# The final norm of an expert layer, moved beside the experts and added to an output that holds the bias

## The chip, the core and the metric

One core of one Trainium2 chip runs the whole program. The time is the device time of one execution in microseconds; the kernel before took 1721.29 us (median of three runs, 1720.49 to 1723.58). A core has TensorE (PE, with its weight loads as PEld), VectorE (DVE), ScalarE (ACT), GpSimd (POOL) and SyncE (SP), each with a queue of its own, and 16 DMA engines that serve the queues of SP and POOL here.

## The reference

One decoder layer over 1024 tokens of 1024 values. An attention mixer and a first layer norm give `h`; then a mixture of experts and a second layer norm give the output. Only the last part matters here:

```python
h   = layer_norm(ALPHA * h + mix, ln1_g, ln1_b)
lg  = h @ w_coarse + b_coarse          # 4 groups, the best one is taken
lf  = h @ w_fine[grp] + b_fine         # 8 experts of that group, the best 2 are taken
ffn = sum over the 2 experts of weight * ((silu(h @ w_gate[e]) * (h @ w_up[e])) @ w_down[e])
out = layer_norm(ALPHA * h + ffn, ln2_g, ln2_b)
```

So both experts of a token lie in one group of eight: experts 0 to 7, 8 to 15, 16 to 23 or 24 to 31. A token of group 0 has its whole sum once expert 7 is through.

## The kernel before

The attention and the first norm end near 1050 us. The routing (`out_norm`, `out_route`, `out_rank`, `out_table`, lines 1259 to 1360) writes `h` to `hbuf` and to `ybuf`, and a table in DRAM with the rows and weights of each expert; `idx` is the table read back.

Then 32 experts run one after the other (loop at line 1676), each in 12 steps `k`. An expert takes up to 128 rows. Steps 0 to 7 multiply the rows by 1024 x 1024 gate and up weights, steps 8 to 11 by 512 x 1024 down weights; a step is one weight tile of 128 x 1024. Each float32 tile is split in two: `eh` is a rounded copy (ACT, line 1479) and `el` the remainder (DVE, line 1480); six matmuls per step (line 1497) use `eh` twice and `el` once. The rows are gathered from `hbuf` by POOL (`gather`, line 1372), transposed on PE (line 1460) and split in the same way (`xt`, ACT line 1466, DVE line 1467). After step 7 come `silu` and `turn`: ACT's silu of each half (line 1504), DVE's product (line 1505), PE's transposes (line 1514), ACT's and DVE's split (lines 1516, 1517). After step 11 `put` scales the two banks on ACT (lines 1521, 1522) and POOL adds the rows to `ybuf` by an indirect DMA (line 1523).

PE, DVE, ACT and POOL take their instructions in program order (`MAN`, line 1668). SP's queue is ordered by the framework, which lets a load go ahead when its page is free. `fetch` takes pages from a ring of some 44 (`er`), in which a tile's page serves first for the load and then for its `el`; `prep` (line 1474) makes `eh` and `el` up to three steps ahead, with three buffers for `eh`. `split_rows` of the next expert and `ahead` come behind the matmuls of a step.

The final norm is a list of letters (`TAIL`, line 65; `final`, line 1630). After expert 30 eight blocks of 128 tokens are loaded from `ybuf`; after the last step of expert 31 they are normed by DVE, ACT and POOL together, and written, with the rows of expert 31 left out. Those are gathered, the expert's product is added (`last_add`, line 1625), normed (`finish_rows`, line 1540) and scattered to the output (`put_rows`, line 1549). The gain and bias are spread over the partitions by matmuls during experts 28 and 29 (`final_gb`, line 1558). A loop behind it (line 1713) takes blocks of rows beyond 128 of an expert; here it has no passes.

Of the kernel before, what the change touches and what calls it, by code (L numbers as in the profile page):

```python
# [9 lines left out]
FP = mybir.dt.float32  # L10
FR = mybir.dt.float32r
BF = mybir.dt.bfloat16
# [51 lines left out]
GBL = (22, 0)  # L64
TAIL = {(30, 11): "L0 L1 L2 L3 L4 L5 L6 L7", (28, 2): "K", (28, 4): "K", (29, 2): "K", (29, 4): "K", (31, 9): "P", (31, 11): "S0 V01 S1 N01 U0 A3 S2 V13 D2 G0p A5 S4 N13 V35 R D4 U1 B0p N35 G1p E2 H4 D5 B1p A7 Z A6 V58 U3 G3p D7 N58 E5 U6 G6p E7 B3d C6p F X"}
# [11 lines left out]
def tile_hybrid(ctx: ExitStack, tc: tile.TileContext, x, xT, w_t, w_gate, pos_k, w1_k, w2_k, pos_v, w1_v, w2_v,  # L77
# [744 lines left out]

    ybd = dram.tile([4, 128, 1024], FP, name="ybd")
# [339 lines left out]
    nof, tok8 = (rc_pool.tile([128, NB], FP, name=n) for n in ("nof", "tok8"))  # L1163
    nid = rc_pool.tile([128, NB], I32, name="nid")
    nc.gpsimd.iota(tok8, pattern=[[128, NB]], base=0, channel_multiplier=1, allow_small_or_imprecise_dtypes=True)
# [14 lines left out]
    tab = dram.tile([S * NE, 2], I32, name="tab")  # L1180
    ti = h_pool.tile([128, 512], I32, name="ti", tag="z", bufs=NZ)
    nc.vector.memset(ti, 4096)
    nc.sync.dma_start(tab.rearrange("(p n) c -> p (n c)", p=128), ti)

# [101 lines left out]
    def out_route(b, L):  # L1286
# [8 lines left out]
        nc.vector.tensor_scalar(e4, e4, sc_[:, 1:2], None, op0=OP.is_equal)  # L1295
        nc.vector.tensor_scalar(e4, e4, -1.0, 1.0e30, op0=OP.add, op1=OP.mult)
# [21 lines left out]
        nc.vector.tensor_tensor(nof[:, b:b + 1], oh[:, 0, NE - 1:NE], oh[:, 1, NE - 1:NE], op=OP.add)  # L1318
# [94 lines left out]

    nc.vector.scalar_tensor_tensor(nid, nof, 4096.0, tok8, op0=OP.mult, op1=OP.add)
# [12 lines left out]
    nc.vector.tensor_copy(ntot, CX[:, 31:32])  # L1427
# [112 lines left out]
    def finish_rows(pl, z, o, g2, b2):  # L1540

        def centre(mean):
            nc.vector.scalar_tensor_tensor(o, z, mean, g2, op0=OP.subtract, op1=OP.mult)
        r, _, _ = stats(pl, z, EPS / ALPHA ** 2, centre, ((0, 512), (512, 1024)))
        for i in range(2):
            c = slice(i * 512, i * 512 + 512)
            nc.vector.scalar_tensor_tensor(o[:, c], o[:, c], r, b2[:, c], op0=OP.mult, op1=OP.add)

    def put_rows(o, ids, outs=()):
        s_ = nc.gpsimd.indirect_dma_start(out=out[0], out_offset=bass.IndirectOffsetOnAxis(ap=ids, axis=0), in_=o,  # L1550
                                          in_offset=None, bounds_check=S - 1, oob_is_err=False)
# [4 lines left out]
    zs = {}  # L1556

    def final_gb():

        kept.extend([next(er_at) for _ in range(3)])  # L1560
        gb, *ts = (p(n) for p, n in zip(kept, ("gb", "g2", "b2")))
        for i, src in enumerate((ln2_g, ln2_b)):
            nc.sync.dma_start(gb[32 * i:32 * i + 1, :], bass.AP(tensor=src.tensor, offset=src.offset,
                                                              ap=[[0, 1], [1, 1024]]))
        yield
        for i, t in enumerate(ts):
            for h in range(2):
                c, ps = slice(h * 512, h * 512 + 512), bank("pt")
                nc.tensor.matmul(ps, ones[32 * i:32 * i + 1, :], gb[32 * i:32 * i + 1, c], start=True, stop=True)
                nc.scalar.copy(t[:, c], ps)  # L1570
                yield ts

    def final_load(b):
        zs[b] = er("zf")
        nc.sync.dma_start(zs[b], ybuf[b * 128:b * 128 + 128, :])

    def final_stats(b):
        bs = fmt[:, b, 2:14].rearrange("p (a b) -> p a b", a=2)
        for i in range(2):
            nc.vector.bn_stats(bs[:, i], zs[b][:, i * 512:i * 512 + 512])  # L1580
        nc.vector.bn_aggr(fmt[:, b, 0:2], fmt[:, b, 2:14])

    def final_stats_act(b):

        os_[b] = er("of")
        mean, var, s1 = fmt[:, b, 0:1], fmt[:, b, 1:2], fmt[:, b, 2:3]
        nc.scalar.activation(os_[b], zs[b], AF.Copy, scale=1.0 / D, accum_out=mean)
        nc.scalar.activation(os_[b], zs[b], AF.Square, scale=-1.0, bias=mean, accum_out=s1)
        nc.scalar.activation(var, s1, AF.Copy, scale=1.0 / D)

    def final_root(a, n):
        root(fmt[:, a:n], *(fmv[:, i, a:n] for i in range(3)), EPS / ALPHA ** 2)

    def final_newton(a, n):
        newton(fmt[:, a:n], *(fmv[:, i, a:n] for i in range(4)))

    def final_unit(b):
        nc.scalar.activation(zs[b], zs[b], AF.Identity, scale=fmv[:, 1, b:b + 1], bias=fmv[:, 3, b:b + 1])

    def final_shift(b):  # L1600
        nc.vector.scalar_tensor_tensor(zs[b], zs[b], fmt[:, b, 0:1], gb[0], op0=OP.subtract, op1=OP.mult)

    def final_scale(b, skip=False):
# [4 lines left out]
    def final_gain(b, eng):  # L1608
        eng.tensor_tensor(zs[b], zs[b], gb[0], op=OP.mult)
# [220 lines left out]
```

## Time and profile before

| what | us |
| --- | --- |
| median of the runs | 1721.29 |
| the execution that was profiled | 1719.97 |
| its span, first to last instruction | 1718.2 |
| busy: PE, DVE, ACT, POOL | 1587.5, 1264.3, 1103.8, 439.2 |
| granted TensorE clock, mean | 0.972 |

The profile is one execution taken by the hardware profiler. Times in a row are us from the start of the span; "busy" is the time in which an engine executes. A row of the timeline gives start, duration, engine, line, operation, output and inputs with their shapes, and in brackets how long the engine had stood idle and what released it. Instructions that follow one another closely are one row with a count, and their durations overlap a little, so the distance of the starts is the better price of one. Tiles that share a bank of PSUM carry each other's names: `pt` and `av` at line 1497 are the two banks of gate and up, `sc` those of the down product.

### The profile page before, as it was taken

The numbers are of one execution on the slowest core, as the hardware profiler recorded it, in microseconds if no ns is written. First come the engines' busy times: TensorE is split into PE (matmuls) and PEld (weight loads), VectorE is DVE, ScalarE is ACT, GpSimd is POOL, SyncE is SP. The second block draws the span as 40 slices with busy tenths as digits, with TensorE's granted clock in tenths as the row PEclk, the third lists the DMA queues.
The fourth block names the chain that finished last, engine by engine and source line by source line (L and its number), as shares of the span: only waits on it lengthen the run. The fifth ranks groups of instructions, "written<-read, shape, count | busy, mean of one in ns | idle before, by whom it ended". The sixth has DMA issues, their size and how long they took to land. (4 is left out here: it accounts for less than half of the span.)

```text
span 1718.2 us, 24639 instructions
## 1 busy us (share of the span) xinstructions
PE 1587.5 (92%) x8114; PEld 1310.5 (76%) x8114; DVE 1264.3 (74%) x2680; ACT 1103.8 (64%) x2037; POOL 439.2 (26%) x390
## 2 busy tenths in 40 slices
PE   7999999998899999999799996999999999999970
PEld 6888888777678988788678895777777777777750
DVE  5555553347867774588877797998998899889786
ACT  4566665525557785578933014887887888788772
POOL 1011122341223332323610242221121212113134
PEclk9999999999999999999999997999999999999995
DMA  4111112232320111001356769999999999999532
GB/s 172 38 37 38 37 38 68 74 101 89 123 86 35 36 47 33 25 18 57 96 177 212 292 213 346 353 364 358 362 366 354 367 359 329 370 364 370 164 118 102
DMA packets 104518, 308.85 MB, mean 180 GB/s; under 512 B 20387, under 2 KB 24611, under 8 KB 104388
## 3 DMA queue, kind: packets, MB, share of 16 engines
q1 hardware_dynamic: 94228, 289.25, 46.0%
q0 software_dynamic: 10160, 18.00, 4.2%
q8 instruction: 65, 1.06, 0.3%
q14 instruction: 65, 0.53, 0.1%
HBM read 283.18 MB, written 41.17 MB: 189 GB/s over the span
## 5 line engine op out<-in xcount | busy, mean ns | idle before, releaser
L1480 DVE TENSOR_TENSOR el<-er,eh 128x1024 fp32r<-128x1024 f32 x384 | 448.1, 1219 | 31.7 <-ACT eh L1479 29.8
L1479 ACT CAST eh<-er 128x1024 fp32r<-128x1024 f32 x384 | 391.0, 1056 | 43.8 <-PE pt L1497 29.1
L232 PE MATMUL pp<-xh,wh 128*128 128x512 f32 x672 | 273.7, 407 | 1.6 <-DVE q L287 1.6
L234 PE MATMUL pp<-xh,wl 128*128 128x512 f32 x672 | 265.9, 396 | 0.0
L233 PE MATMUL pp<-xl,wh 128*128 128x512 f32 x672 | 264.4, 393 | 0.0
L1497 PE MATMUL av<-eh,xt 128*128 128x512 f32 x512 | 196.9, 395 | 1.4 <-ACT xt L1466 1.2
L1497 PE MATMUL pt<-eh,xt 128*128 128x512 f32 x512 | 196.2, 393 | 0.0
L1523 POOL DMA_INDIRECT ybuf<-y,idx x30 | 95.9, 3198 | 212.3 <-ACT y L1522 205.6
L234 PEld LDWEIGHTS pp<-xh,wl 128*128 128x128 f32 x672 | 127.1, 189 | 29.7
L232 PEld LDWEIGHTS pp<-xh,wh 128*128 128x128 f32 x672 | 127.5, 190 | 21.1 <-DVE q L287 2.0
L233 PEld LDWEIGHTS pp<-xl,wh 128*128 128x128 f32 x672 | 127.7, 190 | 19.4
L1497 PE MATMUL sc<-eh,at 128*128 128x512 f32 x512 | 141.4, 398 | 0.0
L892 POOL TENSOR_TENSOR pw<-pw,st 128x64 f32<-128x64 f32 (+5 forms) x128 | 85.9, 701 | 183.2 <-DVE st L887 156.5
L1497 PEld LDWEIGHTS av<-eh,xt 128*128 128x128 f32 x512 | 96.4, 188 | 27.8 <-ACT eh L1479 3.0
L1497 PEld LDWEIGHTS pt<-eh,xt 128*128 128x128 f32 x512 | 96.5, 189 | 22.2
L930 DVE TENSOR_TENSOR PT<-pt,PT 128x512 fp32r<-128x512 f32 (+1 forms) x136 | 90.9, 671 | 25.1 <-ACT PT L929 23.6
L1497 PEld LDWEIGHTS sc<-eh,at 128*128 128x128 f32 x512 | 93.6, 188 | 20.1 <-ACT eh L1479 0.4
L1497 PE MATMUL av<-el,xt 128*128 128x512 f32 x256 | 104.6, 409 | 0.0
L1497 PE MATMUL pt<-el,xt 128*128 128x512 f32 x256 | 100.9, 394 | 0.0
L1372 POOL DMA_INDIRECT xg<-hbuf,idx x31 | 33.3, 1075 | 253.3 <-PE pp L1460 239.6
L123 POOL TENSOR_TENSOR wl<-wr,wh 128x1024 fp32r<-128x1024 f32 x24 | 59.0, 2458 | 140.1 <-ACT wh L122 120.5
L929 ACT CAST PT<-pt 128x512 fp32r<-128x512 f32 (+1 forms) x136 | 76.7, 567 | 16.7 <-PE pt L922 15.0
(431 smaller groups left out, 3586.0 us busy)
## 6 DMA issues: line engine op xcount, KB each, us to landing
er<-in_w_gu_dram SPq DMA_DIRECT2D x256, 512.0 KB, 7.7
er<-in_w_dn_dram SPq DMA_DIRECT2D x128, 512.0 KB, 7.2
wr<-in_w_t_dram SPq DMA_DIRECT2D x44, 512.0 KB, 3.3
mgd<-mg SPq DMA_DIRECT2D x32, 256.0 KB, 2.0
G<-mgd SPq DMA_DIRECT2D x32, 256.0 KB, 3.4
xr<-in_xT_dram SPq DMA_DIRECT2D x8, 512.0 KB, 8.7
wo<-in_w_oT_dram SPq DMA_DIRECT2D x8, 512.0 KB, 4.8
wor<-in_w_out_dram SPq DMA_DIRECT2D x8, 512.0 KB, 7.6
```

What stands on the lines that cost most here:

```text
L123: (eng or nc.vector).tensor_tensor(lo, raw, hi.bitcast(FP), op=OP.subtract)
L232: nc.tensor.matmul(ps, wh[:, kk], xh[k][:, c], start=k == 0, stop=False)
L233: nc.tensor.matmul(ps, wh[:, kk], xl[k][:, c], start=False, stop=False)
L234: nc.tensor.matmul(ps, wl[:, kk], xh[k][:, c], start=False, stop=k == 7)
L892: nc.gpsimd.tensor_tensor(t, t, st[:, 1, hi_, i:i + 1].to_broadcast([128, w]), op=OP.mult)
L929: nc.scalar.copy(t[:, 0], src)
L930: nc.vector.tensor_tensor(t[:, 1], src, t[:, 0].bitcast(FP), op=OP.subtract)
L1372: nc.gpsimd.indirect_dma_start(out=t, out_offset=None, in_=hbuf, in_offset=bass.IndirectOffsetOnAxis(ap=ids, axis=0), bounds_check=S - 1, ...
L1479: nc.scalar.copy(wh, r)
L1480: nc.vector.tensor_tensor(wl, r, wh.bitcast(FP), op=OP.subtract)
L1497: nc.tensor.matmul(pss[h], a[j == 1][:, kk], (wl if j == 2 else wh)[:, h], start=o == 0 and j == 0, stop=o == n - 1 and j == 2)
L1523: nc.gpsimd.indirect_dma_start(out=ybuf, out_offset=bass.IndirectOffsetOnAxis(ap=self.ids, axis=0), in_=y, in_offset=None, bounds_check=S ...
```

## The change

The tokens of a group are normed as soon as its experts are through, in blocks of up to 128 rows, while later experts run. A list of the rows of each group is made in expert 1 (`lists`): a count by matmul, eight scatters into a table `tabf`, one load `idf`. Groups 0 to 2 have three blocks each, which begin at the experts in `FIN`; group 3 has two blocks and the rows of expert 30, all normed during expert 31 (`last_roots`, `last_ends`); the rows of expert 31 are normed at the end as before. Every block is spread over hooks of the step loop: `at(i, f)` runs `f` behind step `i`. A block that begins at expert e gathers its rows at step 8 of expert e - 1, takes the mean and the sum of squares on ACT at steps 4 and 6 of expert e, and has its root at step 8: three small DVE operations for a first guess from the bits, then fourteen on POOL. ACT's scaling comes at step 4 of expert e + 1, DVE's product with the gain in two halves at step 6 of experts e + 1 and e + 2. The bias is not added by an engine: eight DMAs write it to every row of the output beforehand, and the scatter of a block adds to it. The rows of experts 30 and 31 are written whole. `kept` takes three pages of the ring in expert 1 and no more in expert 22.

```diff
+NFB = 3, 3, 3, 2
+FIN = {9: (0, 0), 11: (0, 1), 13: (0, 2), 17: (1, 0), 19: (1, 1), 21: (1, 2), 25: (2, 0), 26: (2, 1), 28: (2, 2)}
...
+    for b in range(NB):
+        nc.sync.dma_start(out[0, b * 128:b * 128 + 128, :], bass.AP(tensor=ln2_b.tensor, offset=ln2_b.offset,
+                                                                    ap=[[0, 128], [1, 1024]]))
...
+    def lists():
+        kept.extend([next(er_at) for _ in range(3)])
+        gb[:] = (p(n) for p, n in zip(kept, ("g2", "b2", "any")))
+        for t, src in zip(gb, (ln2_g, ln2_b)):
+            nc.sync.dma_start(t, bass.AP(tensor=src.tensor, offset=src.offset, ap=[[0, 128], [1, 1024]]))
...
+        put = []
+        for b in range(NB):
+            s_ = nc.gpsimd.indirect_dma_start(out=tabf, out_offset=bass.IndirectOffsetOnAxis(ap=at[:, b:b + 1], axis=0),
+                                              in_=nid[:, b, :], in_offset=None, bounds_check=128 * 32 - 1,
+                                              oob_is_err=False)
...
+        nc.sync.dma_start(idf.rearrange("p n c -> p (n c)"), tabf.rearrange("(p n) c -> p (n c)", p=128))
...
+    def fin_mean(z, f):
+        nc.scalar.activation(gb[2], z, AF.Copy, scale=1.0 / D, accum_out=f[:, 0:1])
+
+    def fin_square(z, f):
+        nc.scalar.activation(gb[2], z, AF.Square, scale=-1.0, bias=f[:, 0:1], accum_out=f[:, 1:2])
...
+    def fin_bits(f):
+
+        v, r, t, n = (f[:, i:i + 1] for i in range(2, 6))
+        b = t.bitcast(I32)
+        nc.vector.tensor_scalar(v, f[:, 1:2], 1.0 / D, VE, op0=OP.mult, op1=OP.add)
+        nc.vector.tensor_scalar(b, v.bitcast(I32), 1, None, op0=OP.logical_shift_right)
+        nc.vector.tensor_scalar(r.bitcast(I32), b, -1.0, float(0x5f3759df), op0=OP.mult, op1=OP.add)
+        for _ in range(3):
+            nc.gpsimd.tensor_tensor(t, r, r, op=OP.mult)
+            nc.gpsimd.tensor_tensor(t, t, v, op=OP.mult)
+            nc.gpsimd.tensor_scalar(t, t, -0.5, 1.5, op0=OP.mult, op1=OP.add)
+            nc.gpsimd.tensor_tensor(r, r, t, op=OP.mult)
+        nc.gpsimd.tensor_tensor(t, f[:, 0:1], r, op=OP.mult)
+        nc.gpsimd.tensor_scalar(n, t, -1.0, 0.0, op0=OP.mult, op1=OP.add)
...
+    def fin_unit(z, f):
+        nc.scalar.activation(z, z, AF.Identity, scale=f[:, 3:4], bias=f[:, 5:6])
+
+    def fin_gain(z, c):
+        nc.vector.tensor_tensor(z[:, c], z[:, c], gb[0][:, c], op=OP.mult)
...
+    def take(ids):
+        b = dict(z=er("zf"), f=fin_new())
+        rows_of(b["z"], ids)
+        return b
+
+    def block(n, ids):
+
+        b = {}
+        at(n - 4, lambda: b.update(take(ids)))
+        at(n + 4, lambda: fin_mean(b["z"], b["f"]))
+        at(n + 6, lambda: fin_square(b["z"], b["f"]))
+        at(n + 8, lambda: fin_bits(b["f"]))
+        at(n + 16, lambda: fin_unit(b["z"], b["f"]))
+        at(n + 18, lambda: fin_gain(b["z"], slice(0, 512)))
+
+        def end():
+            fin_gain(b["z"], slice(512, 1024))
+            outs.append(put_rows(b["z"], ids, outs, compute_op=OP.add))
+        at(n + 30, end)
+
+    steps_ = lists()
+    for i in (13, 16, 17, 18, 19):
+        at(i, lambda: next(steps_, None))
+    le = 12 * NE - 12
+    for e, (c, i) in FIN.items():
+        block(12 * e, idf[:, 8 * c + i, 0:1])
...
+    def last_roots():
+        fin_moments(lb[0]["z"], lb[0]["f"])
+        for i in (1, 2):
+            last_var(lb[i])
+        for i in (1, 2, 0):
+            fin_guess(lb[i]["f"])
+        for i in (1, 2):
+            fin_newton(lb[i]["f"])
+            fin_unit(lb[i]["z"], lb[i]["f"])
+
+    def last_ends():
+        fin_shift(lb[0]["z"], lb[0]["z"], lb[0]["f"])
+        fin_newton(lb[0]["f"])
+        for i in (1, 2):
+            fin_gain(lb[i]["z"], all_)
+            outs.append(put_rows(lb[i]["z"], ids_[i], outs, compute_op=OP.add))
+        fin_scale(lb[0]["z"], lb[0]["f"])
+        put_rows(lb[0]["z"], ids_[0], outs)
+    for i in range(3):
+        at(le - 4 + i // 2, lambda i=i: lb.update({i: take(ids_[i])}))
+    at(le - 1, lambda: [add_rows(lb[0]["z"], lb[0]["z"], ex[NE - 2], h) for h in range(2)])
+    for i in (1, 2):
+        at(le + 2 * i - 1, lambda i=i: fin_mean(lb[i]["z"], lb[i]["f"]))
+        at(le + 2 * i, lambda i=i: fin_square(lb[i]["z"], lb[i]["f"]))
+    at(le + 8, last_roots)
+    at(le + 9, last_ends)
...
+    at(le + 7, lambda: (rows_of(zg, last.ids), nc.scalar.preload_act_table_set(LNEXP)))
+    at(le + 11, final)
```

## Rows read from the trace of the kernel before

**Rows 1.** Busy us by stretch: PE, PEld, DVE, ACT, POOL, then clock, DMA share, GB/s.
```profile
1300.00:1400.00 100.00, 98.70 (x447) 77.44 (x445) 89.39 (x98) 82.90 (x108) 24.06 (x11) 1.00 0.99 363
...
1660.00:1680.00 20.00, 4.04 (x17) 2.67 (x15) 18.99 (x33) 13.32 (x26) 9.00 (x4) 0.73 0.67 247
1680.00:1700.00 20.00, 0.00 (x0) 0.00 (x0) 19.86 (x18) 5.42 (x10) 14.71 (x7) 0.50 0.35 141
```

**Rows 2.** Timeline of PE at its end: the last two matmuls.
```profile
1663.47 0.62 PE L1497 MATMUL sc<-el,at 128*128 128x512 f32 x2
```

**Rows 3.** Timeline of the tail: DVE at the rows of expert 31, POOL's last scatter.
```profile
1683.56 1.39 DVE L1628 SCALAR_TENSOR_TENSOR zl<-sc,idx,xg 128x512 f32<-128x512 f32 x2
...
1698.58 1.27 DVE L1190 BATCH_NORM_STATS2 bs<-zl 128x6 f32<-128x512 f32 x2
...
1701.77 0.16 DVE L1210 SCALAR_TENSOR_TENSOR mv<-mv 128x1 f32<-128x1 f32 x1
1701.96 1.42 DVE L1547 SCALAR_TENSOR_TENSOR ol<-ol,mv,b 128x512 f32<-128x512 f32 x2
1703.65 0.98 POOL L1550 DMA_INDIRECT out_dram<-ol,idx  x1 [4.14 <-DVEq L1713]
```

**Rows 4.** Timeline of ACT in one expert: the last casts and the silu.
```profile
1308.14 1.05 ACT L1479 CAST eh<-er 128x1024 fp32r<-128x1024 f32 x1 [0.34 <-PE pt L1497]
1309.52 1.05 ACT L1479 CAST eh<-er 128x1024 fp32r<-128x1024 f32 x1 [0.33 <-PE pt L1497]
1312.08 0.39 ACT L1504 ACTIVATE act<-av 128x256 f32<-128x256 f32 x1 [1.50 <-PE av L1497]
```

**Rows 5.** Timeline of DVE in the same expert: from step 2 to the silu.
```profile
1302.39 8.05 DVE L1480 TENSOR_TENSOR el<-er,eh 128x1024 fp32r<-128x1024 f32 x7
1310.61 1.23 DVE L1480 TENSOR_TENSOR el<-er,eh 128x1024 fp32r<-128x1024 f32 x1 [0.16 <-ACT eh L1479]
1312.49 0.42 DVE L1505 TENSOR_TENSOR act<-act,av 128x256 f32<-128x256 f32 x1 [0.66 <-ACT act L1504]
1313.20 0.42 DVE L1505 TENSOR_TENSOR act<-act,pt 128x256 f32<-128x256 f32 x1 [0.28 <-ACT act L1504]
```

**Rows 6.** Waits from 1100 to 1600 us: total us, times, longest.
```profile
PEld pt L1514 <- DVE act L1505: 13.3, 27, 0.5
PEld av L1497 <- DVE el L1480: 9.3, 26, 0.4
```

**Rows 7.** Timeline of ACT in the tail: mean, square, and what follows.
```profile
1668.26 1.04 ACT L1587 ACTIVATE of<-zf 128x1024 f32<-128x1024 f32 x1
...
1669.42 1.15 ACT L1588 ACTIVATE of<-zf,fmt 128x1024 f32<-128x1024 f32 x1
...
1670.69 0.20 ACT L1589 ACTIVATE fmt<-fmt 128x1 f32<-128x1 f32 x1
```

**Rows 8.** Timeline of the tail: DVE and POOL passes over 128 x 1024 side by side.
```profile
1688.71 6.65 DVE L1605 SCALAR_TENSOR_TENSOR of<-zf,fmv,b 128x1024 f32<-128x1024 f32 x2
...
1688.63 5.65 POOL L1609 TENSOR_TENSOR zf<-zf,g 128x1024 f32<-128x1024 f32 x2 [1.72 <-ACT zf L1598]
```

**Rows 9.** Groups of POOL over the span by shape: busy us, mean ns, idle before.
```profile
L892 POOL TENSOR_TENSOR pw<-pw,st 128x64 f32<-128x64 f32 x64 | 25.4, 396 | 183.2 <-DVE st L887 156.5 <-ACT PT L929 17.9 <-PE sc L371 7.8
...
L1817 POOL MEMSET const-float32-0.0<- 128x1 f32 x1 | 0.1, 98 | 0.2 <-issue 0.2
```

**Rows 10.** Timeline of SP's queue in the first 60 us.
```profile
11.72 0.42 SPq L708 DMA_DIRECT2D rb<-in_b_r_dram  x1
32.43 27.55 SPq L214 DMA_DIRECT2D wr<-in_w_t_dram  x4
```

**Rows 11.** DMA issues over the span: count, and median us to landing.
```profile
ybuf<-y,idx POOLq DMA_INDIRECT x30, 10.1
...
out_dram<-of,nid POOLq DMA_INDIRECT x2, 4.5
```

**Rows 12.** Issues of down weights: duration ns, first and last start us.
```profile
L1528 SPq DMA_DIRECT2D er<-in_w_dn_dram x128: 327/328/1145, 873.7 to 1605.2; - x128
```

More of the change, by code (lines that the diff above doesn't have):

```diff
@@ L1538, in rows_of @@
                                      bounds_check=S - 1, oob_is_err=False)
[L1540 to L1549, printed above, removed]
+    outs, gb = [], []
@@ L1554, in put_rows @@
         return s_
[L1556 to L1578, printed above, removed]
-        for i in range(2):
[L1580 to L1603, printed above, removed]
-        o = os_[b] if b in os_ else er("of")
-        nc.vector.scalar_tensor_tensor(o, zs[b], fmv[:, 1, b:b + 1], gb[1], op0=OP.mult, op1=OP.add)
-        final_put(b, o, skip)
@@ new lines, in fin_guess, with fin_newton @@
+    def fin_guess(f):
+        v, r, t = (f[:, i:i + 1] for i in range(2, 5))
+        nc.scalar.activation(t, v, AF.Ln)
+        nc.scalar.activation(r, t, AF.Exp, scale=-0.5)
+    def fin_newton(f):
+        v, r, t, n = (f[:, i:i + 1] for i in range(2, 6))
+        nc.vector.tensor_tensor(t, r, r, op=OP.mult)
+        nc.vector.scalar_tensor_tensor(t, t, -0.5, v, op0=OP.mult, op1=OP.mult)
+        nc.vector.scalar_tensor_tensor(r, t, 1.5, r, op0=OP.add, op1=OP.mult)
+        nc.vector.scalar_tensor_tensor(n, f[:, 0:1], -1.0, r, op0=OP.mult, op1=OP.mult)
@@ new lines, in fin_unit, with fin_shift, fin_scale @@
+    def fin_unit(z, f):
+        nc.scalar.activation(z, z, AF.Identity, scale=f[:, 3:4], bias=f[:, 5:6])
+    def fin_gain(z, c):
+        nc.vector.tensor_tensor(z[:, c], z[:, c], gb[0][:, c], op=OP.mult)
+    def fin_shift(o, z, f):
+        nc.vector.scalar_tensor_tensor(o, z, f[:, 0:1], gb[0], op0=OP.subtract, op1=OP.mult)
+    def fin_scale(o, f, cut=1):
+        for i in range(cut):
+            c = slice(i * 1024 // cut, (i + 1) * 1024 // cut)
+            nc.vector.scalar_tensor_tensor(o[:, c], o[:, c], f[:, 3:4], gb[1][:, c], op0=OP.mult, op1=OP.add)
@@ new lines, in tile_hybrid, with final @@
+    for i in (1, 2):
[3 more added lines that the diff above has]
+    at(le + 9, last_ends)
+    last, zl = ex[NE - 1], None
+    def final():
+        nonlocal zl
+        zl, ol = er("zl"), er("ol")
+        finish_rows(ol, zl, last, zg)
+        put_rows(ol, last.ids, outs)
+    at(le + 7, lambda: (rows_of(zg, last.ids), nc.scalar.preload_act_table_set(LNEXP)))
+    at(le + 11, final)
@@ L1672, in tile_hybrid @@
     ex[NXG].gather()
-    last = ex[NE - 1]
     zg = XG[NXG - 1]
@@ L1691, in tile_hybrid @@
             ex[e].put()
-        if (e, k) == GBL:
-            gb_ = final_gb()
-            next(gb_)
-        if (e, k) in TAIL:
-            final(TAIL[e, k])
-        if (e, k) == (NE - 2, 11):
-            zl, ol = er("zl"), er("ol")
+        for f in hooks.pop(i, ()):
+            f()
+    assert not hooks
     mo_.close()
```

158 lines of the change are left out of this document (102 added, 56 removed).

## The prediction

> **What bounds the kernel now.** I read the stages first, then the end, then one expert in the middle. The table of stretches [rows 1] shows two regimes. While the experts run, PE is busy 98.70 of 100 us at full clock, with DVE at 89.39, ACT at 82.90 and the DMA engines at 0.99. After them PE stands still and DVE does nearly all: 18.99 and then 19.86 of 20 us. The last matmul starts at 1663.47 and ends at 1664.1 [rows 2]; POOL issues the last scatter at 1703.65, 39.6 us later, and the span ends 14.6 us after that [rows 3]. So the final norm of eight blocks is a tail of 39.6 us on DVE, with the other engines mostly idle. The change moves most of it beside the experts. The question is what it costs there.
>
> Inside an expert PE is not held all the time by itself. Two waits return once per expert [rows 6]: PE waits 0.5 us for the silu product (27 times) and 0.4 us for an `el` (26 times, at the second weight step). Between them DVE is the bound: it starts late after the silu and works without a gap until it has caught up. From that second step to the next silu PE is the bound: DVE gives an `el` each 1.15 us (8.05 for seven), PE takes 1.38 us per step (ACT's casts at 1308.14 and 1309.52 wait 0.34 and 0.33 us for it) [rows 4, 5]. Just ahead of the silu there are holes: ACT waits 0.33 and 1.50 us, DVE 0.66 and 0.28 us [rows 4, 5]. Work put in a hole is free; work that overfills a hole, or lies between the silu and the second step, is paid in full.
>
> **The tail.** Old end: issue at 1703.65. New: four ACT passes for the last blocks (1.16 for a mean, 1.27 for a square, start to start, 4.9 us together [rows 7]) fall into steps 1 to 4 of expert 31, whose slack is four times 0.33 and the 1.50 before the silu, 2.8 us [rows 4]. So the last matmuls come 2.1 us later, and the last `el` at about 1665.5. Behind it stand on DVE: one pair of half statistics (1.27, and 0.2 to join them), eleven small operations of 0.19 start to start, one shift, four more small ones, two gains of 1.15, one scale; I price shift and scale at 1.2 each, between the 1.15 of a plain pass and the 1.42 of the last scaling in two halves [rows 3, 5]. That is 9.0 us, and 0.5 for handing the root to ACT and back: 1675.0. Then the rows of expert 31: 1.39 for the sum, and the stretch that the old kernel has from 1698.58 to 1703.38, 4.8 us [rows 3]: 1681.2. The last scatter writes rows that the one before may also write, so it waits for that one to land. That one is free at 1675, behind two adding scatters on POOL; I put its issue at 1677.6, and with 4.5 us to landing [rows 11] the last one goes at 1682.1. **Gain 21.5 us.** Adding scatters land in 10.1 us under load [rows 11]; the last one does not wait for them, so both ends of that cost lie off the path. The drain of 14.6 us stays.
>
> **Taken out of the experts:** four broadcast matmuls of 512 columns, at a sixth of a step (1.38 / 6 = 0.23): **0.9 us gained**. The eight row loads and stores of the tail go with it.
>
> **The lists** in expert 1: 31 small DVE operations of 0.19 us, 5.9 us in steps 1 to 6. DVE's room there is 0.23 per step for seven steps and the holes of 0.16, 0.66 and 0.28: 2.7 us. **Cost 3.2 us.** The eight table scatters are POOL's, which is busy a quarter of the time [rows 1]. SP's load of the finished table waits for them; ahead of it the weights lie fetched far in advance (below).
>
> **The bias fill:** eight DMAs without a dependence. SP does not keep program order: the load of the router bias, line 708, goes out at 11.72 us, and after it SP has nothing until 32.43 us [rows 10]. I expect the fills there, under the first projections; 4 MB in that hole is 0 us. Bounds: none gained, and if the next weight tile queues behind their end, some 3 us lost.
>
> **The nine blocks**, each spread over three experts. (a) Mean and square, 2.43 us, meet ACT holes of 1.83: the silu starts 0.6 late, its second half, which has 0.3 of waiting of its own, 0.26 late. PE waits for the second half, so 0.3 per block. (b) The unit pass, 1.16 into a hole of 0.33, makes the eighth cast and its `el` 0.8 late; the half gain behind it (0.6, half of an `el`) would have fitted DVE's 0.66, but now the product comes 0.8 late, its second half 0.5: 0.5 per block. (c) The second half gain alone costs 0, covered by the 0.66; where it meets (a) in one expert (experts 11, 13, 19, 21, 28) that expert loses 0.45 in place of 0.26. Experts 26 and 27, with two blocks at once, I place at 1.65 and 1.1. Sum over the experts: 3 x 0.26 + 5 x 0.45 + 7 x 0.5 + 1.65 + 1.1 = 9.3. (d) The three small operations that seed the root stand on DVE between the silu and the second step: 3 x 0.19 = 0.57, paid in full. (e) Then fourteen single-column operations on POOL. No row has these. The nearest are a one-column memset of 0.098 us and a 64-column product of 0.396 [rows 9]; I take 0.1 to 0.2, near the memset, since a column is what they have. Two of them fall between DVE passes of the bound stretch, 0.2. Together (d) and (e) 0.77 x 9 = 6.9. **Cost 16.2 us.** Further ends: nothing but (d), if PE has slack that these rows do not show, 5 us; and the rival of POOL's chain.
>
> **Sum:** -21.5 - 0.9 + 3.2 + 16.2 = -3.0 against the execution profiled, 1719.97 us (span 1718.2): 1717.0. The median of the runs shown, 1721.29, is 1.3 us above that execution. 1717 is 0.25% below the median; 0.2%, 3.4 us, is about what a measurement of this kernel can tell from no change.
>
> **Rival 1: POOL's chain is not ready when ACT wants it, and the kernel gets slower.** In the tail two POOL passes and two DVE passes, issued together, took 5.65 and 6.65 us [rows 8], where two `el`s, of the same width, take 2.3 [rows 5]: they alternate, each waiting for a whole instruction of the other. If a one-column operation must also wait for the DVE pass that runs, POOL gets one in per DVE instruction. Between the seeds and the moment ACT reaches the unit pass, 9.3 us, DVE has nine instructions queued (two `xt`, seven `el`), so nine of fourteen are through, or twelve if the short `xt` let more by. The others come with the next `el` and in the pause behind it: the unit pass is 1.4 to 2.8 us late, and since the holes are already filled, so is the silu. Nine times that is 13 to 25 us: 1730 to 1742. It decides as soon as an operation takes more than 9.3 / 14 = 0.66 us. For it: rows 8. Against: no single-column operation has been seen waiting. Chance 0.30. The Trainium skill has the same as a rule (SBUF — State Buffer, section Who interferes with whom): a DVE instruction with two SBUF inputs contends with a GpSimd instruction that reads SBUF, and one with at most one SBUF input does not. By it the `el`s block POOL and the `xt`, which read PSUM, do not; rows 8 agree for passes of full width, and no run here shows it for one column.
>
> **Rival 2: the passes are hidden.** If the holes take all ACT and DVE passes and only the seeds cost (9 x 0.57 = 5), the sum is -21.5 - 0.9 + 3.2 + 5 = -14: 1706, and 1703 with the lists free as well. For it: DVE idles 10.6% and ACT 17% in this stage [rows 1]. Against: the two waits of rows 6, which leave no room in half of each expert. Chance 0.22.
>
> **Rival 3: the weights come late.** The DMA engines stand at 0.99 and 363 GB/s [rows 1]; each block adds a gather and an adding scatter, by estimate 85 rows of 4 KB moved three times, 9.4 MB over nine blocks or 26 us at 363 GB/s, and holds a page of the weight ring for some 34 steps. But the last weight load is issued at 1605.2 [rows 12], 58 us before PE uses the last, so 26 us fit in the lead. If they did not, 1743. The skill's estimating figure for HBM to SBUF (same page, Summary: rules for kernel authors), about 358 GB/s, says that there is no room at all; by it the sum would be 26 us more once the lead is spent. Chance 0.05.
>
> **How the numbers follow.** The forecast, 1717, has 0.43; its own range is 1710 to 1725 (tail by 3 either way, blocks by 5), which gives faster 0.24, same 0.14, slower 0.05. Rival 2 adds 0.22 to faster, rivals 1 and 3 0.35 to slower. So faster 0.46, same 0.14, slower 0.40. The range of 1703 to 1738 leaves out the upper part of rival 1, rival 3, and a little under rival 2.
>
> **What would show it.** Right: the last scatter some 16 us after the last matmul, not 39.6; expert for expert a silu that comes 0.3 to 0.5 us later where (a) or (b) lies; ACT's unit pass starting without a wait. Wrong: ACT waiting for POOL ahead of the unit pass (rival 1); block experts no longer than the others (rival 2); casts waiting for weight DMAs after expert 9 (rival 3); or the last scatter waiting for an adding one, or weight tiles behind the fills in the first 40 us, which would undo the first and the fourth step.

## The result, and the profile after

The changed kernel takes 1738.41 us (median of four, 1735.59 to 1744.47), the kernel before 1720.89 beside it: ratio 1.0108, interval 1.0073 to 1.0143. It is slower, by 1.1%. The forecast was 1717, and its range ended at 1738. Rival 1 happened, and its 1730 to 1742 hold the time.

The execution profiled is the longest of the four (1744.47, span 1742.7). Its first silu stands at 1073.1, 5.0 later than in the profile of before. Over the kernels below, which hardly differ up to there, that point lies anywhere from 1062.8 to 1073.1, so these 5 us are spread between executions and no part of the change.

Where the rest went is read from a clock that the kernel carries itself: the second silu of each expert on ACT. Two neighbours lie 18.82 us apart where nothing is added. The timeline of ACT after the change, experts 8 to 11 (second silu only):

```profile
1227.71 0.38 ACT L1509 ACTIVATE act<-pt 128x256 f32<-128x256 f32 x1 [0.31 <-PE pt L1502]
...
1246.54 0.38 ACT L1509 ACTIVATE act<-pt 128x256 f32<-128x256 f32 x1 [0.17 <-PE pt L1502]
...
1266.49 0.37 ACT L1509 ACTIVATE act<-pt 128x256 f32<-128x256 f32 x1
...
1288.03 0.38 ACT L1509 ACTIVATE act<-pt 128x256 f32<-128x256 f32 x1 [0.17 <-PE pt L1502]
```

From expert 8 to 9 it is 18.83, although the mean and the square of the first block lie there: they cost nothing. Then come 19.95 and 21.54: the block costs 1.13 and 2.72 us. Read so over all experts, the excess over 18.82 is 4.0 us for the lists (intervals 0 and 1) and 42.6 us for the nine blocks (intervals 9 to 30; an interval has the number of the expert that it begins with). Of these, 1.2 us in interval 30 belong to the new tail, since **none** below, which has no blocks, keeps them. In the kernel before only intervals 27 and 28 are longer, by 2.52 and 2.53: the broadcast of gain and bias, which the change removes. From the last of these silus to the end of the span it is 39.4 us, before 61.6. So 42.6 + 4.0 - 5.05 - 22.2 = +19.4, which with the 5.0 us at the start is the difference of the two profiled spans (24.5); the medians differ by 17.5.

The table of stretches after the change (PE, PEld, DVE, ACT, POOL, clock, DMA share, GB/s):

```profile
1300.00:1400.00 100.00, 94.44 (x421) 74.13 (x420) 85.63 (x98) 80.76 (x106) 40.62 (x35) 0.98 0.96 355
1500.00:1600.00 100.00, 85.63 (x381) 67.52 (x380) 77.33 (x87) 73.76 (x97) 34.14 (x34) 0.95 0.97 367
```

Against [rows 1] every engine but POOL is less busy: the experts wait. The waits after the change, 1060 to 1700 us (total, times, longest), say on what:

```profile
PEld av L1519 <- DVE act L1510: 39.7, 17, 11.5
...
ACT zf L1667 <- POOL fm L1652: 16.5, 9, 1.9
...
ACT any L1623 <- DMA zf<-ybuf,idf: 9.1, 2, 7.8
```

The second line is the forecast's own sign of rival 1: ACT's unit pass (its scaling of a block's rows) waits for POOL's chain, 1.9 us in eight of the nine blocks and 1.3 in that of expert 26. Of the third, 7.8 us are one block, that of expert 26. The first is where both arrive: PE's transposes behind the silu, which waited at most 0.5 us before [rows 6].

**Inside POOL's chain.** The timelines of POOL and of DVE from the silu of expert 9 to that of expert 10, after the change:

```profile
1253.29 0.20 POOL L1647 TENSOR_TENSOR fm<-fm 128x1 f32<-128x1 f32 x1 [3.67 <-DVE fm L1645]
1253.56 0.19 POOL L1648 TENSOR_TENSOR fm<-fm 128x1 f32<-128x1 f32 x1
1253.84 1.14 POOL L1649 TENSOR_SCALAR fm<-fm 128x1 f32<-128x1 f32 x1
1255.06 0.19 POOL L1650 TENSOR_TENSOR fm<-fm 128x1 f32<-128x1 f32 x1
1255.33 0.20 POOL L1647 TENSOR_TENSOR fm<-fm 128x1 f32<-128x1 f32 x1
1255.61 1.10 POOL L1648 TENSOR_TENSOR fm<-fm 128x1 f32<-128x1 f32 x1
1256.80 1.05 POOL L1649 TENSOR_SCALAR fm<-fm 128x1 f32<-128x1 f32 x1
1257.93 1.05 POOL L1650 TENSOR_TENSOR fm<-fm 128x1 f32<-128x1 f32 x1
...
1263.62 0.20 POOL L1651 TENSOR_TENSOR fm<-fm 128x1 f32<-128x1 f32 x1
1263.91 0.19 POOL L1652 TENSOR_SCALAR fm<-fm 128x1 f32<-128x1 f32 x1
```

```profile
1253.12 0.68 DVE L1472 TENSOR_TENSOR xt<-pp,xt 128x512 fp32r<-128x512 f32 x1
1253.71 1.22 DVE L1485 TENSOR_TENSOR el<-er,eh 128x1024 fp32r<-128x1024 f32 x1
1254.85 0.68 DVE L1472 TENSOR_TENSOR xt<-pp,xt 128x512 fp32r<-128x512 f32 x1
1255.45 8.05 DVE L1485 TENSOR_TENSOR el<-er,eh 128x1024 fp32r<-128x1024 f32 x7
1266.34 1.23 DVE L1485 TENSOR_TENSOR el<-er,eh 128x1024 fp32r<-128x1024 f32 x1 [2.85 <-ACT eh L1484]
1267.49 0.68 DVE L1670 TENSOR_TENSOR zf<-zf,g 128x512 f32<-128x512 f32 x1
```

Lay the two side by side. While an `xt` runs (one input from PSUM), POOL's operation of one column takes 0.19 to 0.20 us, two of them in one `xt`. While an `el` runs (both inputs from SBUF) it takes 1.05 to 1.14 and ends just after the `el`. During the row of seven it gets one operation in per `el`; when they are over, it is back at 0.20. DVE pays nothing: seven `el`s take 8.05 us, as in [rows 5]. The chain takes 10.8 us, from 1253.29 to 1264.10. The Trainium skill's rule (SBUF — State Buffer, section Who interferes with whom), which the forecast gave with rival 1, holds here for a single column too.

What follows on ACT, and the product on PE's path, in the timeline of ACT:

```profile
1261.19 1.05 ACT L1484 CAST eh<-er 128x1024 fp32r<-128x1024 f32 x1 [0.33 <-PE pt L1502]
1264.13 1.24 ACT L1667 ACTIVATE zf<-zf,fm 128x1024 f32<-128x1024 f32 x1 [1.90 <-POOL fm L1652]
1265.28 1.03 ACT L1484 CAST eh<-er 128x1024 fp32r<-128x1024 f32 x1
```

The last cast stands behind the unit pass, so DVE is idle for 2.85 us ahead of its `el` (0.16 before [rows 5]), the half gain stands behind that, and the product behind both. The silu is 1.13 late and the product later still, which the next interval shows: 1.5 us in intervals 14 and 20, and 2.6 to 2.7 in 10, 12, 18 and 22. What makes the second kind dearer is the granted clock of TensorE. PE stands still for 2.3 us in each of them, waiting for the product. Here are PE's first transposes behind that stand in the first block, the stretch that follows them, and the same stretch for the block that begins at expert 13 (columns as in the table of stretches above):

```profile
1268.55 0.44 PE L1519 MATMUL av<-ident,act 128*128 128x128 f32 x2 [2.33 <-DVE act L1510]
...
1269.10:1272.10 3.00, 3.00 (x11) 2.61 (x10) 2.09 (x4) 2.59 (x5) 1.04 (x1) 0.50 1.04 322
1352.00:1355.00 3.00, 3.00 (x17) 2.36 (x16) 1.94 (x4) 2.87 (x5) 1.07 (x1) 1.00 1.05 359
```

At the end of the stand or shortly behind it the granted clock falls to 0.50 in the first case, the lower of its two levels (1.2 GHz), and stays at 1.00 in the second (2.4 GHz). A stretch at the lower level lasts 3.4 us here, and a block with one costs some 1.2 us more. In the nine blocks PE stands for 2.3 to 2.4 us eight times; five of these stands are followed by such a stretch and three are not. What decides between them is not shown by these runs.

**Expert 26** has interval 25 longer by 11.2. POOL's and ACT's timelines:

```profile
1585.88 0.19 POOL L1652 TENSOR_SCALAR fm<-fm 128x1 f32<-128x1 f32 x1
1586.74 1.04 POOL L1541 DMA_INDIRECT zf<-ybuf,idf  x1 [0.67 <-DMA er<-in_w_gu_dram]
```

```profile
1595.12 1.06 ACT L1623 ACTIVATE any<-zf 128x1024 f32<-128x1024 f32 x1 [7.77 <-DMA zf<-ybuf,idf]
```

Here two blocks begin in neighbouring experts. The gather of the second stands on POOL behind the chain of the first, and ACT's mean waits 7.77 us for it, with the casts and the silu behind the mean. PE stands for 11.3 us, and from within that stand on the clock is at 0.50 for 10.2 us.

**Lists, fills, tail**, after the change: DVE in expert 1, SP in the first 60 us, and PE, POOL and DVE at the end.

```profile
1092.74 0.18 DVE L1583 TENSOR_SCALAR blk<-pp 128x32 f32<-128x32 f32 x1
...
1095.97 0.15 DVE L1598 CAST ntot<-more 128x1 int32<-128x1 f32 x1
1096.04 0.41 DVE L1510 TENSOR_TENSOR act<-act,av 128x256 f32<-128x256 f32 x1
```

```profile
12.12 0.42 SPq L708 DMA_DIRECT2D rb<-in_b_r_dram  x1
12.60 9.77 SPq L824 DMA_DIRECT2D out_dram<-in_ln_b_dram  x8
34.98 14.46 SPq L214 DMA_DIRECT2D wr<-in_w_t_dram  x3
```

```profile
1711.20 0.73 PE L1502 MATMUL sc<-el,at 128*128 128x512 f32 x2
...
1722.57 1.01 POOL L1610 DMA_INDIRECT out_dram<-zf,idx  x1 [0.30 <-issue]
...
1725.16 1.41 DVE L1678 SCALAR_TENSOR_TENSOR ol<-ol,fm,b 128x512 f32<-128x512 f32 x2
...
1729.26 0.99 POOL L1610 DMA_INDIRECT out_dram<-ol,idx  x1 [5.68 <-DMA out_dram<-zf,idx]
```

Of the lists' 31 operations 18 stand in one row ahead of the silu's product, 3.3 us; PE stands for 3.1 us behind them, and in this execution its clock stays at 1.00. The fills lie where the forecast put them. The last scatter goes 18.1 us after the last pair of matmuls starts; before it was 40.2 [rows 2, 3]. It still waits 5.68 for the scatter of expert 30's rows to land, and DVE is done 2.7 us earlier.

### The profile page after: what moved, and what is told of

The parts are those of the page before. It is cut to its first block, busy times and chain, and to the rows that moved or that the text cites. A ratio compares the mean times of both kernels' runs of the same rounds, so it can differ in the third digit from the quotient of the medians.

```text
span 1742.7 us, 24909 instructions
## 1 busy us (share of the span) xinstructions
PE 1600.2 (92%) x8109; PEld 1321.7 (76%) x8109; DVE 1256.2 (72%) x2738; ACT 1119.7 (64%) x2062; POOL 529.5 (30%) x544
## 5 line engine op out<-in xcount | busy, mean ns | idle before, releaser
L1502 PE MATMUL sc<-eh,at 128*128 128x512 f32 x512 | 147.2, 410 | 0.1
L232 PEld LDWEIGHTS pp<-xh,wh 128*128 128x128 f32 x672 | 127.9, 190 | 21.1 <-DVE q L287 2.0
L1528 POOL DMA_INDIRECT ybuf<-y,idx x30 | 74.8, 2494 | 152.4 <-ACT y L1527 69.0
L439 POOL TENSOR_TENSOR oT<-U 64x256 f32<-64x256 f32 x48 | 35.5, 739 | 169.0 <-DVE U L425 164.0
```

The costliest lines, as they stand in the source:

```text
L232: nc.tensor.matmul(ps, wh[:, kk], xh[k][:, c], start=k == 0, stop=False)
L439: nc.gpsimd.tensor_tensor(ov, i0, i1, op=OP.add)
L1502: nc.tensor.matmul(pss[h], a[j == 1][:, kk], (wl if j == 2 else wh)[:, h], start=o == 0 and j == 0, stop=o == n - 1 and j == 2)
L1528: nc.gpsimd.indirect_dma_start(out=ybuf, out_offset=bass.IndirectOffsetOnAxis(ap=self.ids, axis=0), in_=y, in_offset=None, bounds_check=S ...
```

## The experiments

Theory: the cost is POOL's chain being late for ACT. Rivals: the passes themselves, the gathers, the fills. Each result is the median in us, then its ratio to the kernel before, which ran beside it (its medians were 1717.87 to 1720.27), with the ratio's 95% interval.

**none.** No blocks at all: the rows of groups 0 to 2 are not normed.

```diff
-FIN = {9: (0, 0), 11: (0, 1), 13: (0, 2), 17: (1, 0), 19: (1, 1), 21: (1, 2), 25: (2, 0), 26: (2, 1), 28: (2, 2)}
+FIN = {}
```

> The nine blocks of groups 0 to 2 are left out (their rows keep the bias alone); lists, bias fill and the new tail stay. By the spacing of the silus in the profile of the changed kernel the nine blocks add 42 us there; so both theories expect about 1697 to 1702 us, some 38 to 42 below the changed kernel, and equal spacing of the silus (18.8 us) from expert 3 to expert 29. If the loss lay in lists, fill or tail instead, this kernel would stay above 1720.

1697.88 us, 0.9857 (0.9822 to 0.9891). Intervals 9 to 29 are back at 18.82; interval 30 keeps 1.2. So the blocks cost 40.5 us, and all the rest of the change gains 21.1: in this profile tail 22.4 (23.6 less the 1.2 of interval 30) and broadcast 5.05, less 6.2 for the lists, which cost 1.10 and 5.12 here. That leaves next to nothing for the fills. The lists are the same code as in the changed kernel, and PE stands for the same 3.1 us, but here the clock falls to 0.50 for 6.8 us; in **two** it does for 3.4 us, and the interval costs 4.1 in place of 2.9 or 5.1.

**two.** Two Newton steps on POOL in place of three (a less exact root), ten operations in place of fourteen.

```diff
-        for _ in range(3):
+        for _ in range(2):
```

> Two Newton steps on POOL in place of three: the chain has 10 operations, not 14. Theory (the unit pass waits for the chain): the chain takes about 6.5 us in place of 10.8, the 1.9 us wait of the unit pass is gone in all nine blocks, and the gather of block 26, which stands behind the chain of block 25 on POOL, comes 4 us earlier: 17 to 24 us less than the changed kernel, about 1715 to 1721 us. Rival (the ACT and DVE passes overfill their holes, and the chain does not matter): at most 3 us less, 1735 or more.

1718.59, 0.9999 (0.9984 to 1.0014). Four small operations per block are worth twenty microseconds. ACT's wait for POOL is gone from the list of waits, and with it the five stretches at the lower clock in intervals 10, 12, 18, 22 and 29; five of the six blocks in experts 9 to 22 cost 0.6 to 0.8 (the first 0.46 and 0.18, in intervals 9 and 10). Interval 25 is still 8.3 too long; ACT waits 6.9 us there for the gather.

**early.** The gather one step earlier, ahead of the neighbour's chain on POOL.

```diff
-        at(n - 4, lambda: b.update(take(ids)))
+        at(n - 5, lambda: b.update(take(ids)))
```

> Each block's rows are gathered one step earlier, so that the gather of the block at expert 26 goes ahead of the POOL chain of the block at expert 25. Theory (the one long stall, 7.8 us of ACT in expert 26, is this order on POOL): the interval from silu 25 to silu 26 falls from 30 to about 22 us, and the time by 7 to 9 us, to about 1730. Rival (the DMA engines are late there, whatever the order): the stall stays, no change.

1731.97, 1.0065 (1.0042 to 1.0089). Interval 25 falls from 11.18 to 3.84; the other blocks keep their cost, and so does the wait for POOL (17.0 us, nine times). In that interval the gather's place was worth 7.3 us; the whole gained 6.4, since intervals 27 to 30 grew from 8.7 to 11.3. What the other blocks cost is not the gather's.

**fill_late.** The bias fills go out at 377 us, long after the start.

```diff
+    with tc.issue_after(mgs[-1].ins):
+        for b in range(NB):
+            nc.sync.dma_start(out[0, b * 128:b * 128 + 128, :], bass.AP(tensor=ln2_b.tensor, offset=ln2_b.offset,
+                                                                        ap=[[0, 128], [1, 1024]]))
```

> The eight bias fills are held in SP's queue until the last store of the gates, far behind the start. Theory (the fills delay the third weight tile and cost 2 us in the first 15 us): the first matmul groups run as in the kernel before and the time falls by 2 us, to about 1736. Rival (the shift at the start is spread of the first executions): no change. A loss would mean that the fills stand in the way of weight tiles wherever they are.

1741.85, 1.0115 (1.0089 to 1.0142): nothing gained. Its first silu is at 1072.4, as late as with the fills at the start. The theory fell and the rival held: moving the fills gains nothing, **none** leaves no cost for them, and the later start of that execution is not theirs.

**unit_late.** The unit pass two steps later, directly ahead of the silu; the first half gain at the next expert's end.

```diff
-        at(n + 16, lambda: fin_unit(b["z"], b["f"]))
-        at(n + 18, lambda: fin_gain(b["z"], slice(0, 512)))
+        at(n + 18, lambda: fin_unit(b["z"], b["f"]))
+        at(n + 29, lambda: fin_gain(b["z"], slice(0, 512)))
```

> Chain of 14 as in the changed kernel; the unit pass comes two steps later, at step 6, in front of the silu, where ACT has a hole of 1.5 us, and the first half gain at step 5 of the expert after. Theory (the unit pass arrives before the chain ends): the chain ends 1.9 us after the old place of the unit pass, and step 6 lies 2.8 us behind it, so the wait is gone without a shorter chain: 10 to 17 us less than the changed kernel, 1721 to 1728. Rival (the passes overfill their holes): no gain, since the same passes lie in the same experts.

1732.8, 1.008 (1.0063 to 1.0097), less than expected. Two reasons show in its trace: the silu now stands right behind the unit pass, which still waits for POOL up to 1.4 us (behind the silu of expert 9 the chain ends at 1259.70, and ACT has stood idle for 1.34), and interval 25 has 11.8 (interval 27 grows to 6.4). A block in experts 9 to 22 costs 1.1 to 2.5, where it cost 2.7 to 3.9. The wait was moved and nearly halved (9.5 us in all, from 16.5), not removed.

**on_dve.** The three steps on DVE (ten operations), none on POOL.

```diff
-            nc.gpsimd.tensor_tensor(t, r, r, op=OP.mult)
-            nc.gpsimd.tensor_tensor(t, t, v, op=OP.mult)
-            nc.gpsimd.tensor_scalar(t, t, -0.5, 1.5, op0=OP.mult, op1=OP.add)
-            nc.gpsimd.tensor_tensor(r, r, t, op=OP.mult)
...
+            nc.vector.tensor_tensor(t, r, r, op=OP.mult)
+            nc.vector.scalar_tensor_tensor(t, t, -0.5, v, op0=OP.mult, op1=OP.mult)
+            nc.vector.scalar_tensor_tensor(r, t, 1.5, r, op0=OP.add, op1=OP.mult)
```

> The three Newton steps run on DVE (ten more operations of one column at 0.19 us behind the three seeds) and nothing on POOL. It measures the step that priced operations between the silu and the second weight step in full. If they are paid in full, each block costs 1.9 us more than in the kernel with two steps on POOL (1718.6): 1732 to 1736, with no wait of the unit pass for POOL. If DVE has room there after all: 1712 to 1720.

1731.13, 1.006 (1.0037 to 1.0083). DVE's timeline behind the silu of expert 9, first and last of the thirteen, and the `xt` behind them:

```profile
1251.82 0.15 DVE L1643 TENSOR_SCALAR fm<-fm 128x1 f32<-128x1 f32 x1
...
1254.12 0.16 DVE L1650 SCALAR_TENSOR_TENSOR fm<-fm 128x1 f32<-128x1 f32 x1
1254.20 0.69 DVE L1472 TENSOR_TENSOR xt<-pp,xt 128x512 fp32r<-128x512 f32 x1
```

They hold the `xt` up by 2.4 us between the silu and the second step, and a block costs 2.6 to 3.9 (intervals 9 to 22). Three of the six blocks there cost 2.6 to 2.7, about 2.0 above the 0.6 to 0.8 of **two**, which is the ten operations: work in that stretch is paid in full, as the forecast said of the seeds. The other three cost 3.8 to 3.9, and in each of them the clock is at 0.50 for 3.4 us.

**best.** Two steps (as in **two**), the gather early, and no dependence between a group's gathers and the adding scatters of later groups, whose rows are others.

```diff
-        at(n - 4, lambda: b.update(take(ids)))
+        at(n - 5, lambda: b.update(take(ids, grp)))
...
+            for g, p in takes:
+                if g < e // 8:
+                    tc.declare_no_dep(s_.ins, p.ins, reason="rows of another group")
```

> Two Newton steps, the rows gathered one step earlier, and no dependence between the gathers of a group and the adding scatters of experts of later groups (other rows of the same buffer). Theory (the long interval between the silus 25 and 26, 8.3 us over the others with two steps, is the chain gather, scatter, gather, in which each waits some 10 us for the landing of the one before): that interval falls to 1 us over the others, and the time to 1709 to 1712, 7 to 10 us below the kernel before. Rival (the DMA engines have no room there): the interval keeps most of its 8 us, 1715 or more.

1715.53, 0.998 (0.9967 to 0.9994): faster than before, but less so than expected. Interval 25 is down to 1.3; how much of that is the dependence and how much the shorter chain was not separated. What is left is 6.3 in the lists, and 9.5 in intervals 27 to 30 (1.2 of them the tail's). In SP's list stands a wait that the kernel before does not have:

```profile
SPq L1533 <- DMA out_dram<-zf,idf: 33.3, 4, 10.7
```

SP cannot load a weight into a page until a block's scatter out of that page has landed. The changed kernel has more of it (79.6 us, seven times), but there no cast waits for a weight once the blocks have begun.

**before_dma.** The kernel before, with gain and bias spread by two DMAs, and without the four matmuls and their copies.

```diff
-        for i, src in enumerate((ln2_g, ln2_b)):
-            nc.sync.dma_start(gb[32 * i:32 * i + 1, :], bass.AP(tensor=src.tensor, offset=src.offset,
-                                                              ap=[[0, 1], [1, 1024]]))
...
-                nc.tensor.matmul(ps, ones[32 * i:32 * i + 1, :], gb[32 * i:32 * i + 1, c], start=True, stop=True)
-                nc.scalar.copy(t[:, c], ps)
...
+        for t, src in zip(ts, (ln2_g, ln2_b)):
+            nc.sync.dma_start(t, bass.AP(tensor=src.tensor, offset=src.offset, ap=[[0, 128], [1, 1024]]))
```

> The kernel before, with the gain and the bias spread over the partitions by two DMAs in expert 22 and without the four matmuls and the copies of experts 28 and 29. The intervals of the silus in the kernel before are 2.5 us longer in each of these experts; if the matmuls and copies are the cause, all intervals become equal and the time falls by 5 us, to 1714. By the price in the prediction (four matmuls at 0.23 us) it falls by 0.9 us, to 1718.

1714.42, 0.9975 (0.9962 to 0.9988). No interval is longer than 18.86: by the intervals the broadcast alone cost 5 us, by the medians 4, and not 0.9. Leaving it out gains as much as **best** does in all. The trace of the kernel before already held the price:

```profile
1587.81 0.39 PE L1497 MATMUL pt<-el,xt 128*128 128x512 f32 x1
1588.13 1.12 PE L1569 MATMUL pp<-gb,ones 1*128 1x512 f32 x2
1589.18 0.50 PE L1497 MATMUL av<-eh,xt 128*128 128x512 f32 x1
```

One broadcast matmul (one input row of plain float32 data) is two records on PE and takes 1.05 us to the start of the next matmul, where one of the experts' matmuls, also of 512 columns but of 128 input rows and rounded data, takes 0.23. It puts that next matmul off by 1.14 us, so four make 4.6 of the 5.05. Whether the single input row or the type of the data makes it dear was not tried.

**ahead.** As **best**, but with all three steps; mean, square and seeds one, one and two steps earlier, and the gather one more.

```diff
-        at(n + 4, lambda: fin_mean(b["z"], b["f"]))
-        at(n + 6, lambda: fin_square(b["z"], b["f"]))
-        at(n + 8, lambda: fin_bits(b["f"]))
+        at(n + 3, lambda: fin_mean(b["z"], b["f"]))
+        at(n + 5, lambda: fin_square(b["z"], b["f"]))
+        at(n + 6, lambda: fin_bits(b["f"]))
```

> All fourteen POOL operations of a block stay (three Newton steps), but the mean, the square and the seeds of the root come one, one and two steps earlier, so that the seeds stand ahead of the silu and the chain has some 5 us more before ACT reaches the unit pass; the gather is one step earlier still, and free of the adding scatters of later groups. If the cost was only that the chain was late, the wait of ACT's unit pass for POOL goes to zero with all fourteen operations, the block experts fall to the 0.2 to 0.6 us of the version with two Newton steps, and the time is 1713 to 1718. If the cost is the operations themselves (they hold up DVE or another engine whenever they run), the block experts keep 1.1 to 2.7 us and the time is 1728 to 1735.

1716.16, 0.9994 (0.9981 to 1.0006). This settles it: all fourteen operations are there, the chain ends before ACT asks, and the wait is gone. POOL's last operation for the first block, and ACT's unit pass in expert 10:

```profile
1253.75 0.19 POOL L1652 TENSOR_SCALAR fm<-fm 128x1 f32<-128x1 f32 x1
```

```profile
1262.56 1.24 ACT L1667 ACTIVATE zf<-zf,fm 128x1024 f32<-128x1024 f32 x1
```

Interval 9 has no excess left and interval 10 has 0.20. It is not the operations that cost, but that they end after ACT has done its cast and asks. The longest interval that is left has another reason: 22 has 5.23, where a cast waits 3.6 us for a down tile, which the next runs come to.

**spread** and **both.** The lists one operation at a time behind steps 2 to 6 of experts 1 to 7; and that together with the order of **ahead** and two steps.

```diff
-    for i in (13, 16, 17, 18, 19):
+    for i in [13] + [12 * e + k for e in range(1, 8) for k in (2, 3, 4, 5, 6, 6)]:
```

> The version with two Newton steps and earlier, freed gathers, and the lists no longer made in five portions in expert 1, but one small DVE operation behind each of the steps 2 to 6 of experts 1 to 7 (two behind step 6). If the lists cost what they do because fourteen of their operations stand in one row ahead of the silu's product, the 5.2 us of the interval from expert 1 to 2 and the 1.1 before it fall to under 1 us in all, and the time is 1709 to 1711. If small DVE operations cost their time wherever they stand, 6 us are merely spread, and the time stays at 1715.

> Two Newton steps, seeds ahead of the silu, earlier and freed gathers, lists spread. If seeds ahead of the silu fall into the hole of 0.66 us there, the 0.57 per block are saved too, 4 to 5 us over nine blocks, and the time is 1705 to 1708; if the hole is filled already (mean and square lie there too), it is the time of the version with spread lists within 2 us.

1717.87, 0.9998 (0.9986 to 1.001), and 1719.09, 1.0011 (0.9997 to 1.0026). The lists' own cost fell from 6.3 to 1.4 and, in **both**, interval 9, which has the seeds, from 0.46 to nothing, yet the time did not fall below that of **best**. ACT's waits in **both**:

```profile
ACT eh L1484 <- DMA er<-in_w_dn_dram: 11.3, 8, 3.0
```

Single down tiles are late, by 0.9 to 3.0 us, in experts 12, 14, 20, 22 and 29: each three experts behind the start of a block (9, 11, 17, 19 and 26), which is about one round of the ring. The first three of them are issued at 1281.66, 1322.83 and 1437.90; a block's scatter lands at 1281.24, 1322.78 and 1437.83.

**own.** As **both**, with three pages kept out of the ring for the blocks.

```diff
+            if len(own) < 3:
+                own.append(next(er_at))
+                kept.append(own[-1])
+            z = own[nown[0] % 3]("zf", FP)
+            nown[0] += 1
```

> The version with everything earlier (two Newton steps, seeds ahead of the silu, freed gathers, spread lists), and the rows of the blocks of groups 0 to 2 in three pages that are taken out of the ring of weight pages for good, instead of a page of the ring for each block. There four single down tiles were late (ACT's cast waited 2.96, 2.21, 1.46 and 2.77 us for them, and the intervals of experts 12, 20, 22, 27 and 29 are 1.8 to 4.2 us too long) while the other weights had a lead of about 40 us. If such a tile is late because its page was still held by a block until its scatter had landed, the waits are gone with pages of their own, some 15 us are saved against that version, and the time is 1703 to 1707. If the weights are late because the DMA engines have too much to move, a ring shorter by three pages makes it no better: casts still wait for weights, and the time stays at 1715 to 1721.

**1703.63, 0.9901 (0.9882 to 0.9921)**: faster than both kernels, by 17 us than the one before and by 35 than the change. Intervals 9 to 25 have at most 0.44 each. The same wait, and the issue of the down weights (duration, first and last start):

```profile
ACT eh L1484 <- DMA er<-in_w_dn_dram: 1.3, 1, 1.3
```

```profile
L1533 SPq DMA_DIRECT2D er<-in_w_dn_dram x128: 327/328/1157, 870.9 to 1649.3; - x128
```

In SP's list no load of a weight waits for a scatter any more. It was the page, not the load on the DMA engines. The intervals show some 9 of the 15 us between the medians of **both** and **own**: the execution of **both** that was profiled (1712.47) was the fastest of its twelve. That load is to be seen too: the last down tile is issued 24.9 us before the last pair of matmuls (1674.21) starts, 58 before the change [rows 2, 12]. The lead has shrunk by 33 us, where the forecast had 26 for the blocks' rows alone; by estimate three pages fewer in the ring take some 5 of the 33 (three steps of 18.82 / 12). Intervals 28 to 30 still hold 9.2 us: 1.2 of it is the tail's, a part is waits for weights (3.2 in interval 28) and one of 1.9 for a gather, and in interval 29 the clock is at 0.50 for 3.4 us. The rest was not tried.

## Why the prediction was wrong

**The step that failed is (e)**, the price of POOL's fourteen operations. It took 0.1 to 0.2 us for each, from a memset and a product that had run without `el`s beside them [rows 9], and counted two. Alone they do take 0.19; beside an `el` they take 1.05 to 1.14, and eight of the fourteen stand beside one, so the chain took 10.8 us where the forecast had 9.3 for it. The forecast had the limit (more than 0.66 us each and the unit pass is late) and the mechanism, with rows of full width as its only evidence [rows 8]; it gave them a chance of 0.30 because no single column had been seen waiting. The nearest row by width was not the nearest by what ran beside it.

**Rival 1** was right in place, sign and size: nine waits of 1.3 to 1.9 us, 16.5 in all, where it had 1.4 to 2.8 and 13 to 25. The delay is paid at about its length where the clock stays at 1.00: such a block costs 2.7, and 0.7 of that stays when the chain is ready. Where the stand of PE is followed by a stretch at 0.50 it costs 3.7 to 3.9, which neither the forecast nor the rival had. That the time lies within the rival's 1730 to 1742 is therefore partly luck: it had neither the 11.2 us of interval 25 nor some 6 us for the five stretches at the lower clock, and (a) to (d) were priced some 8 us too high.

**Not foreseen:** the order of POOL's queue in expert 26. The forecast placed expert 26 at 1.65 by counting passes, and did not ask what the second gather stands behind. It cost 11.2, of which **early** gave back 7.3.

**(a) to (d)**, read where the chain is ready (**two**, **ahead**, **own**), were priced too high rather than too low: mean and square 0 instead of 0.3 (interval 8); the unit pass with the first half gain 0 to 0.3 instead of 0.5 (first intervals of the blocks in **own**); the interval behind, with the second half gain, 0.2; the seeds 0.2 to 0.45 instead of 0.57 (**two** against **own**). Without the chain, blocks would have cost about 6 us plus expert 26, not 16.2.

**The tail** was right: 22.2 gained, or 21.0 less the 1.2 of interval 30, against 21.5, with the last scatter waiting for the one before it, as said. **The fills** were right at 0. **The lists** were too low: 3.2, against 4.0 here and 6.2 in **none**, because the room of single steps was added up, while 18 of the 31 operations stand in one place; the 2.2 between the two are the clock behind the stand of PE. **The broadcast** was mis-sized: 0.9 for the PE time of four matmuls, 5.05 measured; each holds PE for 1.05 us, not a sixth of a step. These two errors partly cancel.

**Rival 2** would have been near without the chain: **none** shows a gain of 21.1 for everything else, and a block whose chain is ready costs some 0.7. **Rival 3** fell for the change itself: casts waited 0.7 us for weights, all of it ahead of the first block. Late weights came only when the other waits were gone, and mainly through held pages, not through bandwidth.

## What to carry to other kernels

Price a small operation by what runs beside it, not by its own size; where its result is needed by a certain step, compare the end of the whole chain with that step, and start it earlier or shorten it. When TensorE is made to stand, look at its granted clock behind the stand: the stand can cost more than its length. Take the price of a matmul from one of the same shape and type of data, or from its own row. When work is moved into a full pipeline, list for each queue what now stands behind it, gathers included. When a buffer is borrowed from a ring, count hold time plus landing against one round of the ring; the first waits removed will uncover it.

## What the runs showed of the hardware

- One-column operations on POOL: 0.19 us alone or beside an `xt`, 1.05 to 1.14 beside an `el`; the `el`s beside them keep their 8.05 us for seven.
- Two such operations pass in one `xt` of 0.68 us, but one per `el` of 1.22 in a row of seven.
- At or behind the end of a stand of PE of 2.3 to 2.4 us the granted clock fell to 0.50 (1.2 GHz) for 3.4 us in five of eight cases of the changed kernel, and stayed at 1.00 (2.4 GHz) in three. With a stand of 3.1 us at the lists it stayed at 1.00 in the changed kernel and was 0.50 for 3.4 us in **two** and for 6.8 in **none**, and the interval cost 2.9, 4.1 and 5.1 us.
- A matmul of one input row of plain float32 data and 512 columns held PE for 1.05 us in two records, where one of 128 input rows of rounded data held it for 0.23. Four of them, with their copies on ACT, cost the experts 5.05 us, some 2.5 in each of two.
- Down tiles whose page a block had held were issued within 0.5 us of the landing of the block's scatter, and came 0.9 to 3.0 us late; with three pages of their own for the blocks that wait fell from 11.3 us to 1.3.
